# A late pair of loads moved to the weights' queue, and three short matmuls added in the first two tails

## The chip, the cores and the metric

The kernel runs on one core of a Trainium2 chip. Such a core has a matrix engine (TensorE, here PE), a vector engine (VectorE, DVE), a scalar engine (ScalarE, ACT), a general one (GpSimd, POOL) and one that mostly issues transfers (SyncE, SP). Transfers between the chip's large memory and the core run on 16 DMA engines. SP's transfers go through one hardware queue (q1 in the profile), those that POOL issues through a software queue (q0). Matmuls write to a small accumulation memory (PSUM), which ACT and DVE read.

The metric is the time of one execution on the device in microseconds (us), the median of the runs. Lower is better.

## The reference

One layer of a decoder trunk over 512 tokens of width 2048, all in float32. What matters here is its first and its last product:

```python
h = rmsnorm(x, g_mix)
z = einsum('bsd,dc->bsc', h, w_in)          # conv B, C, V | attention Q, K, V | forget logits | two gates
...                                          # gated short convolution and forgetting attention, merged
x = x + einsum('bsd,de->bse', merged, w_mix_out)
h = rmsnorm(x, g_mlp)
u = square(relu(einsum('bsd,df->bsf', h, w_ff1)))     # 2048 -> 8192
x = x + einsum('bsf,fd->bsd', u, w_ff2)               # 8192 -> 2048, "the second MLP matrix"
return rmsnorm(x, g_final)
```

## The kernel before

**Seven products for eight.** Every large product is cut into 2 by 2 blocks and made with seven block products instead of eight (Strassen's scheme in Winograd's form). They are called A11, A12, S1, S2, S3, S4 and A22. Each multiplies a sum of data blocks, which is kept ready in memory, by a sum of weight blocks, which DVE makes when the weights have come.

**Three passes.** Float32 accuracy is had from a shorter format by splitting each operand into a high and a low part. ACT writes the high part (`th`, line 111), DVE the low part (`tl`, line 114), and PE multiplies high by high, high data by low weights or the other way round, and low by high: three matmuls for each pair of blocks. So PE's work on one block product, called a run here, is 48 matmuls of 256 columns, or 24 of 512 columns in the second MLP matrix.

**Two forms.** `mm_cols` (lines 154 to 180) has the weights' parts standing in the array and streams the data through; its three matmuls are lines 171, 175 and 177. `mm_rows` (lines 182 to 201) has the data standing and streams the weights' parts; its matmuls are lines 195, 197 and 199. Both take `extra`. With `extra == "first"` they issue one more matmul of 192 columns ahead of a run's first one, into the same accumulator. It begins the accumulation, and the real first matmul begins it again, so its result is thrown away (line 164 in `mm_cols`, line 193 in `mm_rows`). Some later groups have another kind of short matmul, into a spare bank (line 1058).

**The first stage.** A `Group` is one slab of weight columns with its seven runs: `head` is A11 and A12, `tail2` is S1, S3, S2, S4 and A22 in this order. `heads` is a list of five groups: `gV0`, which makes half of the attention's values and uses `mm_rows`, and four groups for keys and queries, which use `mm_cols` and have `extra={"S3": "first"}`. First all five heads run, then the five tails in the same order. So the first tail is `gV0`'s and the second that of `heads[1]`. Their accumulators are named a, b, c and d: S1 goes to c, S3 to d, S2 to a, S4 to c again, A22 to d again.

**The second MLP matrix.** Its data, the squared activations, are made in the stage before (`ff1`), summed into the seven data blocks and stored to DRAM (`s_d`, lines 1481 and 1482). The last stage reads them back as `us` tiles, at line 1605, in `load_sums`: four tiles for each of eight segments of 1024 rows. For the first segment they take over buffers as the stage before lets go of them: tile 0 (A11, A12) before the last `ff1` group's tail, tile 1 (S2, S3) behind that tail. The last two, tile 2 (S1, A22) and tile 3 (S4), are called the late sums here. They are issued within the first unit, behind its run A12 in the order of the program. Each tile of two blocks is two transfers of 1024 KB, tile 3 two of 512 KB.

A `unit` is one segment by half of the output columns. It loads four weight tiles `y` of 1024 KB on SP (line 1706), in the order (0,0), (1,0), (0,1), (1,1); the fourth is called y11 below. Then it runs A11, A12, S2, S3, S1, A22, S4. Three sums of weights come between: `X[0,1] - X[0,0]`, then `t2 = X[1,1] - ...` for S2, then one for S3.

**Order.** The instructions of each engine run in the order in which a scheduler put them at build time. It follows the program's order as far as it holds a tile's buffers free in time. A transfer is issued by its engine in that order and waits there until its target buffer is free.

Of the kernel before, what the change touches and what calls it, by code (L numbers as in the profile page):

```python
# [8 lines left out]
F32 = mybir.dt.float32  # L9
# [36 lines left out]
def tile_hybrid_block(ctx: ExitStack, tc, x, g_mix, w_in, b_f, b_gate, conv_w, w_conv_out,  # L46
                      w_attn_out, w_mix_out, g_mlp, w_ff1, w_ff2, g_final, out):
    nc = tc.nc
    x, out = x[0], out[0]
# [35 lines left out]
    s_d = [dram.tile([P, 2, 4, 7, HS], F32, name=f"s_d{i}") for i in range(DFF // 1024)]  # L85
# [30 lines left out]
    def split(src, hi, lo):  # L116
        return high_of(src, hi), low_of(src, hi, lo)
# [15 lines left out]
    def parts(shape, at=0):  # L133

        q, w = shape[1:]
        return tuple(main.tile([P, WBUF], F32R, tag=tag, name=tag, bufs=2)[:, at:at + q * w]
                     .rearrange("p (q c) -> p q c", q=q) for tag in ("th", "tl"))
# [44 lines left out]
    def mm_rows(ps, Sx, hi, lo, first, extra=None, blocks=range(2), qs=None):  # L182

        nq, w = hi.shape[1], hi.shape[2]
        for b in blocks:
            o = ps[b][:, :w] if len(ps) == 2 else ps[0][:, b * w:(b + 1) * w]
            begin = first and (b == 0 or len(ps) == 2)
            ts = slice(b * P, (b + 1) * P)
            for part in range(2):
                for q in qs or range(nq):  # L190
                    Sh, Sl = (e[:, ts] for e in Sx(q))
                    if extra == "first" and part == 0 and q == 0 and b == 0:
                        nc.tensor.matmul(o[:, :192], Sh, hi[:, q, :192], start=True, stop=False, skip_group_check=True)
                    if part == 0:
                        tied(nc.tensor.matmul(o, Sh, hi[:, q, :], start=begin and q == 0, stop=False,  # L195
                                              skip_group_check=True))
                        tied(nc.tensor.matmul(o, Sl, hi[:, q, :], start=False, stop=False, skip_group_check=True))  # L197
                    else:
                        tied(nc.tensor.matmul(o, Sh, lo[:, q, :], start=False, stop=q == nq - 1,  # L199
                                              skip_group_check=True))  # L200
# [7 lines left out]
    def moving(t):  # L208

        return lambda q: (t[:, 0, q, :], t[:, 1, q, :])  # L210
# [411 lines left out]
    def store_v(c0, w):  # L622
        def put(i, j, v):
            c = c0 + j * w
            n = min(w, AW - c)
            nc.gpsimd.dma_start(out=v_d[2 * i:2 * i + 2, :, c:c + n].rearrange("t p c -> p t c"), in_=v[:, :, :n])
            if n < w:
                add(fl[:, 2 * i:2 * i + 2, :], v[:, :, n:], bf.unsqueeze(1).to_broadcast([P, 2, NH]))
        return put
# [8 lines left out]
    gV0 = Group(w_in, COL_AV, COL_AV + VW, VW, Q1.moving, mm_rows, ((4,), (3,), (6,), (7,)), store_v(0, VW), shift=3 * SHIFT)  # L638

    def kq(hp, banks):  # L640
        return Group(w_in, COL_K + hp * HS, COL_Q + hp * HS, HS, Q1.moving, mm_cols, banks, store_kq(hp), QSCALE,
                     extra={"S3": "first"})
# [8 lines left out]
    heads = [gV0] + [kq(hp, ((a,), (3,), (6,), (7,))) for hp, a in enumerate((0, 1, 2, 5))]  # L651
# [163 lines left out]

    gV0.after["S2"] = fourth
    gV0.paced = True
    for g in heads:
        g.tail2()
        if g is gV0:  # L820
            ph.close()
# [774 lines left out]

    US = ((4, ("A11", "A12")), (3, ("S2", "S3")), (1, ("S1", "A22")), (2, ("S4",)))

    def load_sums(seg, ks, ST):

        for k in ks:
            place, names = US[k]
            t = main.tile([P, 2, 4, len(names), HS], F32R, tag=f"t{place}", name="us")
            for e in range(2):
                nc.gpsimd.dma_start(out=t[:, e].bitcast(F32), in_=s_d[seg][:, e, :, 2 * k:2 * k + len(names)])
            for e, n in enumerate(names):
                ST[n] = moving(t[:, :, :, e])

    for g in range(1, DFF // S):
        group = ff1(g, ((2 + 2 * (g % 2),), (3,), (1 if g < DFF // S - 1 else 2,), (7,)))  # L1610
        group.head(True, order=((0, 0), (0, 1), (1, 0)))
        if g == DFF // S - 1:
            us0 = {}
# [74 lines left out]
    def banks2(i, name):  # L1688
        return tuple(pairs.tile([P, S], F32, tag=f"q{i}{e}", name=name) for e in range(2))

    def unit(seg, cg, ST):

        a, d = banks2(cg, "a"), banks2(1 - cg, "d")
        if seg == 0:
            kept[cg] = banks2(2 + cg, "b")
        b = kept[cg]
        X, at = {}, {}
        end = seg == NSEG - 1 and cg == 1  # L1700
        for i, j in ((0, 1), (1, 1), (0, 0), (1, 0)) if end else ((0, 0), (1, 0), (0, 1), (1, 1)):
            at[i, j] = free.pop(0)
            t = main.tile([P, 4, S], F32, tag=f"x{at[i, j]}", name=f"y{i}{j}")
            c = NW * cg + S * j
            src = w_ff2[seg * 1024:(seg + 1) * 1024, c:c + S].rearrange("(q two p) c -> two p q c", two=2, p=P)
            nc.sync.dma_start(out=t, in_=src[i])
            X[i, j] = t

        def run(ps, n, src, first):
            hi, lo = parts([P, 4, S])  # L1710
            split(src, hi, lo)
            mm_rows(ps, ST[n], hi, lo, first)

        last = seg == NSEG - 1
        begun = set()

        def into(i, j, ps, end=False):
            for e in range(2):
                xs = place(i, j, cg, e)[2]
                if last and end:  # L1720
                    finish(i, j, cg, ps, e)
                elif seg == 0 and (i, j) not in begun:
                    nc.scalar.activation(out=xs, in_=ps[e], func=AF.Copy)
                elif (i, j, cg) in in_rows:
                    onto_rows(i, j, cg, ps, e)
                else:
                    add(xs, ps[e], xs)
            begun.add((i, j))

        t2 = main.tile([P, 4, S], F32, tag="t0", name="t2")  # L1730
        if end:


            one = const.tile([P, 1], F32, name="one")
            nc.vector.tensor_copy(one, turned[:, 0:1])
            sub(t2, X[1, 1], X[0, 1])
            run(a, "A11", X[0, 0], True)
            onto_rows(0, 0, cg, a, 1)
            onto_rows(0, 0, cg, a, 0, one)
            nc.vector.memset(one, 1.0)  # L1740
            run(d, "S3", t2, True)
            sub(X[0, 0], X[0, 1], X[0, 0])
            sub(X[0, 1], X[1, 1], X[0, 0])
            into(1, 1, d)
            run(a, "S2", X[0, 1], False)
            sub(X[0, 1], X[1, 0], X[0, 1])
            into(1, 0, a)
            for t in (2, 3):
                gain(t, one)
            run(d, "A22", X[0, 1], False)  # L1750
            into(1, 0, d, True)
            run(a, "S1", X[0, 0], False)
            into(1, 1, a, True)
            p4 = (main.tile([P, 4, S], F32R, tag="t0", name="th4"),
                  main.tile([P, 4, S], F32R, tag=f"x{at[0, 1]}", name="tl4"))
            split(X[1, 1], *p4)
            for t in (2, 3):
                Final(t).all()
            p2 = parts([P, 4, S])
            split(X[1, 0], *p2)  # L1760
            for t in (0, 1):
                gain(t, one)
            for e in range(2):
                mm_rows(b, ST["A12"], *p2, False, blocks=(e,))
                finish(0, 0, cg, b, e)
                mm_rows(a, ST["S4"], *p4, False, blocks=(e,))
                finish(0, 1, cg, a, e)
                Final(e).all()
            return
        run(a, "A11", X[0, 0], True)  # L1770
        sub(X[0, 0], X[0, 1], X[0, 0])
        into(0, 0, a)
        run(b, "A12", X[1, 0], seg == 0)
        if seg == 0 and cg == 0:
            load_sums(0, (2, 3), us0)
        if last:
            into(0, 0, b, True)
        sub(t2, X[1, 1], X[0, 0])
        run(a, "S2", t2, False)
        sub(X[0, 1], X[1, 1], X[0, 1])  # L1780
        sub(t2, X[1, 0], t2)
        free.append(at[1, 0])
        into(1, 0, a)
        run(d, "S3", X[0, 1], True)
        free.append(at[0, 1])
        into(1, 1, d)
        run(a, "S1", X[0, 0], False)
        free.append(at[0, 0])
        into(1, 1, a, True)
        run(d, "A22", t2, False)  # L1790
        into(1, 0, d, True)
        run(a, "S4", X[1, 1], False)
        free.append(at[1, 1])
        into(0, 1, a, True)
        if 3 <= seg < 7:
            residual(*((0, 0), (1, 0), (1, 1), (0, 1))[seg - 3], cg)

    kept = {}
    for seg in range(NSEG):
        ST = us0  # L1800
        if seg > 0:
            ST = {}
# [36 lines left out]
```

## Time and profile before

| what | us |
|---|---|
| median of 3 runs (2416.66 to 2418.52) | 2417.17 |
| the profiled execution | 2418.55 |
| its span, first to last instruction | 2416.7 |
| PE busy | 2396.0 (99%) |
| DVE busy | 2029.8 (84%) |
| ACT busy | 1205.1 (50%) |
| mean granted clock of PE | 0.998 |

Rows of a stage table read: stretch, its length, then for PE, PEld (PE's weight loads, which run beside its matmuls), DVE, ACT and POOL the busy time and in brackets the number of instructions, then PE's granted clock, the DMA engines' share and GB/s. Rows of a timeline read: start, duration, engine, line, operation, output and inputs, shapes, count, and in square brackets the idle time before it with what ended it. Rows of the chain read: start, length, what. Groups read: line, engine, operation, output and inputs, shapes, count, busy us, mean ns of one, idle us before them. Ends of matmuls are modelled and overlap with the next start; their starts are measured. Data blocks of the first stage show as A and S, those of w_mix_out as M.

### The profile page before, as it was taken

Reading aid. Unit: us, or ns where it says so; the run is one execution under the profiler, and the core shown is the slowest. Engines: PE = TensorE matmul, PEld = TensorE weight load, DVE = VectorE, ACT = ScalarE, POOL = GpSimd, SP = SyncE. Lnnn points to the kernel's source line nnn. Section 1 sums busy time; section 2 is a strip of 40 time slices with the busy share of each in tenths; the row PEclk is TensorE's granted clock in tenths of the full one; section 3 lists DMA queues with packets and bytes.
Section 4 is the critical chain, followed back from the end, with each engine's and each line's share of the span. In section 5 each row is a group of like instructions: output and inputs, shape, how many; then the busy total and the mean of one; then the engine's idle time right before and its main releaser. Section 6 shows DMA issues by size and latency. Waiting matters only on the chain.

```text
span 2416.7 us, 41351 instructions
## 1 busy us (share of the span) xinstructions
PE 2396.0 (99%) x17775; PEld 2259.7 (94%) x17775; DVE 2029.8 (84%) x1683; ACT 1205.1 (50%) x1238; POOL 300.0 (12%) x480
## 2 busy tenths in 40 slices
PE   9999999999999999999999999999999999999998
PEld 9999999999999999899999999999998888888886
DVE  7987677789888768888988889888887888889898
ACT  7444444445545534446665666666664333333334
POOL 1100111121111112023300000000011001100000
PEclk9999999999999999999999999999999999999999
DMA  8664444464565755566956564655678467665662
GB/s 276 187 189 153 150 154 153 153 205 152 178 201 181 259 176 202 179 193 224 324 184 225 199 231 170 224 206 198 233 288 292 168 210 252 218 212 183 232 231 100
DMA packets 279847, 491.98 MB, mean 204 GB/s; under 512 B 11820, under 2 KB 191112, under 8 KB 279280
## 3 DMA queue, kind: packets, MB, share of 16 engines
q1 hardware_dynamic: 226384, 272.71, 35.6%
q0 software_dynamic: 52672, 215.57, 24.4%
q8 instruction: 139, 2.28, 0.4%
q10 hardware_dynamic: 608, 1.06, 0.1%
q14 instruction: 44, 0.36, 0.0%
HBM read 379.70 MB, written 109.07 MB: 202 GB/s over the span
## 4 chain that ended last, share of the span: by engine, by line
PE 90%; DVE 3%; issue 2%; DMA 2%; ACT 1%; POOL 1%; SPq 0%; POOLq 0%; DVEq 0%; ACTq 0%
PE a L171 6%; PE a L175 6%; PE a L177 6%; PE d L171 5%; PE d L175 5%; PE d L177 5%; PE a L197 5%; PE a L195 5%; PE a L199 5%; PE c L177 4%; PE c L171 4%; PE c L175 4%; PE d L199 3%; PE d L195 3%; PE d L197 3%; PE b L171 3%
## 5 line engine op out<-in xcount | busy, mean ns | idle before, releaser
L111 ACT ACTIVATE th<-x 128x2048 fp32r<-128x2048 f32 (+1 forms) x280 | 537.0, 1918 | 486.6 <-DVE x L128 175.5
L114 DVE TENSOR_TENSOR tl<-x,th 128x2048 fp32r<-128x2048 f32 (+2 forms) x282 | 639.5, 2274 | 152.8 <-ACT th L111 149.1
L128 DVE TENSOR_TENSOR x<-x,x 128x2048 f32<-128x2048 f32 (+1 forms) x160 | 366.1, 2288 | 23.0 <-DMA x<-in_w_in_dram 17.6
L111 ACT ACTIVATE th<-y 128x2048 fp32r<-128x2048 f32 (+1 forms) x109 | 185.3, 1701 | 274.2 <-PE a L197 138.8
L114 DVE TENSOR_TENSOR tl<-y,th 128x2048 fp32r<-128x2048 f32 (+1 forms) x109 | 219.0, 2013 | 28.5 <-ACT th L111 28.1
L195 PE MATMUL a<-th,us 128*128 128x512 f32 x512 | 199.3, 389 | 0.4 <-ACT th L111 0.4
L197 PE MATMUL a<-th,us 128*128 128x512 f32 x512 | 199.2, 389 | 0.0
L171 PE MATMUL c<-S,th 128*128 128x256 f32 x848 | 195.9, 277 | 0.0
L175 PE MATMUL c<-S,th 128*128 128x256 f32 x848 | 195.7, 277 | 0.0
L171 PE MATMUL a<-S,th 128*128 128x256 f32 x784 | 182.3, 278 | 0.0
L175 PE MATMUL a<-S,th 128*128 128x256 f32 x784 | 180.7, 276 | 0.0
L171 PEld LDWEIGHTS c<-S,th 128*128 128x128 f32 x848 | 159.3, 188 | 0.0
L175 PEld LDWEIGHTS c<-S,th 128*128 128x128 f32 x848 | 159.3, 188 | 0.0
L171 PEld LDWEIGHTS a<-S,th 128*128 128x128 f32 x784 | 147.2, 188 | 0.6 <-issue 0.5
L175 PEld LDWEIGHTS a<-S,th 128*128 128x128 f32 x784 | 147.3, 188 | 0.5 <-issue 0.5
L199 PE MATMUL a<-tl,us 128*128 128x512 f32 x512 | 136.9, 389 | 0.6 <-DVE tl L114 0.6
L171 PE MATMUL b<-A,th 128*128 128x256 f32 x544 | 126.0, 277 | 1.4 <-ACT th L111 1.4
L171 PE MATMUL a<-A,th 128*128 128x256 f32 x544 | 126.5, 278 | 0.0
L171 PE MATMUL d<-S,th 128*128 128x256 f32 x544 | 126.4, 278 | 0.0
L175 PE MATMUL d<-S,th 128*128 128x256 f32 x544 | 125.7, 277 | 0.0
L171 PE MATMUL d<-A,th 128*128 128x256 f32 x544 | 125.7, 277 | 0.0
L175 PE MATMUL b<-A,th 128*128 128x256 f32 x544 | 125.5, 277 | 0.0
(401 smaller groups left out, 6030.7 us busy)
## 6 DMA issues: line engine op xcount, KB each, us to landing
x<-in_w_in_dram SPq DMA_DIRECT2D x86, 1024.0 KB, 5.9
y<-in_w_ff_dram SPq DMA_DIRECT2D x64, 1024.0 KB, 7.5
x<-in_w_ff_dram SPq DMA_DIRECT2D x60, 1024.0 KB, 8.2
us<-s_d POOLq DMA_DIRECT2D x48, 1024.0 KB, 9.2
s_d<-rh POOLq DMA_DIRECT2D x32, 896.0 KB, 5.4
s_d<-r POOLq DMA_DIRECT2D x32, 896.0 KB, 5.9
x<-in_w_mix_out_dram SPq DMA_DIRECT2D x17, 1024.0 KB, 6.9
g_d<-o POOLq DMA_DIRECT2D x32, 256.0 KB, 2.9
```

The source lines that it names most:

```text
L111: return tied(nc.scalar.activation(out=hi, in_=src, func=AF.Copy))
L114: return tied(nc.vector.tensor_tensor(out=lo, in0=src, in1=hi.bitcast(F32), op=ALU.subtract))
L128: return nc.vector.tensor_tensor(out=out, in0=a, in1=b, op=ALU.subtract)
L171: i = nc.tensor.matmul(o, hi[:, q, js], Sh, start=first and q == 0 and j == 0, stop=False, skip_group_check=True)
L175: nc.tensor.matmul(o, hi[:, q, js], Sl, start=False, stop=False, skip_group_check=True)
L177: i = nc.tensor.matmul(o, lo[:, q, js], Sh, start=False, stop=q == nq - 1, skip_group_check=True)
L195: tied(nc.tensor.matmul(o, Sh, hi[:, q, :], start=begin and q == 0, stop=False, skip_group_check=True))
L197: tied(nc.tensor.matmul(o, Sl, hi[:, q, :], start=False, stop=False, skip_group_check=True))
L199: tied(nc.tensor.matmul(o, Sh, lo[:, q, :], start=False, stop=q == nq - 1, skip_group_check=True))
```

## The change

Two edits. The first adds `extra` to the first two tails: to `gV0` for S1 and S3, and to `heads[1]` for S1 (it has S3 already). That is three more matmuls of 192 columns, the first two of them in `mm_rows`. The second passes a queue to `load_sums` and uses SP for the late sums of the first segment, four transfers; all other `us` loads stay on POOL.

```diff
     gV0.after["S2"] = fourth
     gV0.paced = True
+    gV0.extra = {"S1": "first", "S3": "first"}
+    heads[1].extra = {"S1": "first", "S3": "first"}
     for g in heads:
         g.tail2()
...
-    def load_sums(seg, ks, ST):
+    def load_sums(seg, ks, ST, queue=nc.gpsimd):
 
         for k in ks:
             place, names = US[k]
             t = main.tile([P, 2, 4, len(names), HS], F32R, tag=f"t{place}", name="us")
             for e in range(2):
-                nc.gpsimd.dma_start(out=t[:, e].bitcast(F32), in_=s_d[seg][:, e, :, 2 * k:2 * k + len(names)])
+                queue.dma_start(out=t[:, e].bitcast(F32), in_=s_d[seg][:, e, :, 2 * k:2 * k + len(names)])
...
         run(b, "A12", X[1, 0], seg == 0)
         if seg == 0 and cg == 0:
-            load_sums(0, (2, 3), us0)
+            load_sums(0, (2, 3), us0, nc.sync)
```

## The prediction

> **What bounds the kernel now.** I read the page first: engine shares, then the chain that ended last.
>
> ```profile
> span 2416.7 us, 41351 instructions
> PE 2396.0 (99%) x17775; PEld 2259.7 (94%) x17775; DVE 2029.8 (84%) x1683; ACT 1205.1 (50%) x1238; POOL 300.0 (12%) x480
> PE 90%; DVE 3%; issue 2%; DMA 2%; ACT 1%; POOL 1%; SPq 0%; POOLq 0%; DVEq 0%; ACTq 0%
> ```
>
> TensorE (PE) is the chain for 90% of the span. So the time can fall in two ways only: matmuls follow each other faster, or PE waits less. The change touches one place of each kind. Both are small, and I look at each with the views of its own stretch.
>
> The first place is the pace. The stage table (length, then PE's busy time with its count) holds stretches that are each one run of 48 matmuls of 256 columns; each begins and ends where the timeline starts a new output. The last four rows come from a second and a third table.
>
> ```profile
> 70.85:76.29 5.44, 5.44 (x50) 5.44 (x49) 5.44 (x3) 0.84 (x2) 0.00 (x0) 1.00 0.67 198
> 76.29:81.95 5.66, 5.66 (x51) 5.66 (x49) 4.16 (x4) 1.92 (x1) 0.71 (x1) 1.00 0.13 46
> 110.31:115.98 5.67, 5.67 (x50) 5.67 (x49) 4.62 (x3) 3.56 (x2) 0.00 (x0) 1.00 0.69 217
> 132.94:138.59 5.65, 5.65 (x50) 5.65 (x49) 5.38 (x4) 0.40 (x2) 1.27 (x2) 1.00 0.39 118
> 138.68:144.17 5.49, 5.49 (x51) 5.49 (x50) 4.21 (x2) 3.28 (x2) 0.57 (x1) 1.00 0.81 242
> 144.17:149.61 5.44, 5.44 (x51) 5.44 (x50) 2.89 (x2) 2.45 (x3) 0.00 (x0) 1.00 0.88 256
> 477.75:483.19 5.44, 5.44 (x51) 5.44 (x50) 5.44 (x5) 3.49 (x2) 0.00 (x0) 1.00 0.66 190
> 483.19:488.74 5.55, 5.55 (x52) 5.55 (x50) 5.19 (x6) 1.50 (x4) 0.00 (x0) 1.00 0.79 217
> 76.29:138.59 62.30, 62.30 (x531) 62.30 (x530) 54.04 (x32) 25.94 (x19) 9.17 (x11) 1.00 0.57 174
> 1800.16:1819.00 18.84, 17.20 (x73) 13.28 (x72) 17.49 (x14) 10.94 (x11) 1.11 (x2) 1.00 0.86 296
> ```
>
> The same work takes 5.44 us in one stretch and 5.65 in another, at the full clock (1.00) and with PE never idle: 113.3 or 117.8 ns a matmul. The slow pace begins at 76.29, where the first tail begins, and lasts over both first tails and one run more, 11 runs, to 138.59. Just there stands a short matmul (192 columns) that the kernel already has:
>
> ```profile
> 110.22 0.25 PE L164 MATMUL d<-S,th 128*128 128x192 f32 x1
> 138.59 0.25 PE L164 MATMUL d<-S,th 128*128 128x192 f32 x1
> ```
>
> The one at 110.22 left the pace slow (5.67 behind it), the one at 138.59 ended it (5.49, then 5.44). The groups of 461 to 843 us hold twelve more (ten L1058, two L164), and there nothing is slow: modelled matmuls of 276 ns, against 281 in the two first tails.
>
> ```profile
> L175 PE MATMUL c<-S,th 128*128 128x256 f32 x320 | 73.5, 276 | 0.0
> L1058 PE MATMUL spare<-S,th 128*128 128x192 f32 x10 | 2.5, 248 | 0.0
> L175 PE MATMUL c<-S,th 128*128 128x256 f32 x48 | 11.4, 281 | 0.0
> ```
>
> The second place is a real wait. In the first unit of the second MLP matrix three runs take 18.84 us (last row of the table) where three at 5.44 are 16.32: 2.52 us lost. The chain says to what:
>
> ```profile
> 1784.15 2.30 DVE tl L114
> 1786.47 15.33 DMA y<-in_w_ff_dram
> 1801.82 0.04 DVE t L128
> ...
> 1812.91 2.29 DVE tl L114
> 1815.25 1.20 PE d L199 x4
> ```
>
> The unit's fourth weight tile y11 is 15.33 us on its way, VectorE (DVE) starts S2's sum when it lands, and from there DVE is back to back until PE has what it waited for.
>
> **The change part by part: the three short matmuls.** Price of one: 483.19 to 488.74 is 48 matmuls with a short one ahead, 5.55 against 5.44, so 0.11 us on PE's path; three cost 0.33. Nothing hides it. The weight loads they bring run beside (PEld), and no wait is added: each needs only what the next matmul needs.
>
> Gain, if the pace becomes fast at the first of them: 62.30 less the 0.11 of the short one it holds, less 11 x 5.44, is 2.35 us. Net -2.02. If only the second (first tail, S3) does it, 0.21 less. If only the third or the old one at 110.22 does it, 6 or 5 runs of 0.21 remain: -0.93 or -0.72 net. If none, +0.33. No row shows a short matmul in the row form (gV0's, data as moving operand) nor one where the form changes, so its result is bounded by these: from -2.02 to +0.33, and further up if the later rescue is lost (below). I take -2.02. Twelve short matmuls met a fast pace and left it fast; the first new one stands right behind a fast run (70.85 row). Row-form matmuls can run fast, as those of w_mix_out do (mean 276, in 1065 to 1076 us):
>
> ```profile
> L195 PE MATMUL d<-th,M 128*128 128x256 f32 x16 | 3.7, 276 | 0.0
> ```
>
> Cover when PE gets faster: DVE is the next engine, 54.04 of 62.30 us. At 11 x 5.44 plus four short ones PE needs 60.3, so DVE still fits, and the tails behind 138.59 run at the fast pace with the same DVE work and no wait.
>
> [...]
>
> **The late sums.** POOL (GpSimd) issues them now, and SP (the weights' queue) after the change. Four issues leave POOL, four come onto SP. The listing of POOL, then DVE around the wait, then the issue views of y11, of the early pair and of the S1/A22 pair:
>
> ```profile
> 1784.27 1.52 POOL L1605 DMA_DIRECT2D us<-s_d  x2 [0.48 <-PE d L177]
> 1789.71 1.50 POOL L1605 DMA_DIRECT2D us<-s_d  x2 [3.92 <-PE a L177]
> 1795.15 1.49 POOL L1605 DMA_DIRECT2D us<-s_d  x2 [3.94 <-PE d L177]
> 1808.01 0.56 POOL L1481 DMA_DIRECT2D s_d<-rh  x1 [11.37 <-ACT rh L1478]
> 1801.82 2.29 DVE L128 TENSOR_TENSOR t<-y,y 128x2048 f32<-128x2048 f32 x1 [1.17 <-DMA y<-in_w_ff_dram]
> DMA to landing us min/median/max: 15.3/15.3/15.3
> L1605 POOL DMA_DIRECT2D us<-s_d x2: 766/766/766, 1784.3 to 1785.0; - x2
> DMA to landing us min/median/max: 12.3/14.1/15.8
> DMA to landing us min/median/max: 13.7/14.7/15.7
> ```
>
> SP: y11 is issued at 1786.47; the new loads wait for PE at 1789.71 and 1795.15. Behind them SP has the next unit's weights, which wait for a free buffer until 1813.06:
>
> ```profile
> L1706 SPq DMA_DIRECT2D y<-in_w_ff_dram x1: 368/368/368, 1813.1 to 1813.1; - x1
> ```
>
> 18 us lie between, so the added waits hold up nobody. On POOL the next work waits for ScalarE (ACT) at 1808: nothing is won there.
>
> What y11 wins: in 1790 to 1798 the software queue q0 moved twice what q1 (weights) did, and in 1798 to 1802 q1 finished y11 beside it.
>
> ```profile
> q0 software_dynamic: 539, 2.12, 68.1%
> q1 hardware_dynamic: 493, 0.99, 33.8%
> ...
> q0 software_dynamic: 357, 1.36, 89.8%
> q1 hardware_dynamic: 105, 0.18, 12.9%
> ```
>
> But until about 1800.8 (second early load, issued at 1785.0, 15.8 us on its way) q0 still carries the early pair, which stays on POOL. Only the last 1.0 us of y11 (1800.8 to 1801.8) competes with the late sums alone, at a third of the rate; alone it takes a third, 0.33. Gain 0.67. Upper bound: DVE was idle 1.17 us before that sum and not longer. Lower: 0. I take 0.65, the slowest engine's view, since a landing counts only when all are done. DVE's chain passes it on: S2's th, its tl and S3's tl (1815.2) all come 0.65 earlier, and PE's last wait there (1815.25) is set by that tl. The remaining 1.9 us of waiting stay. The S1/A22 pair lands by 1806.2 now (second issue 1790.5, 15.7 us); S1 starts at 1819, so it has 13 us to spare on either queue.
>
> [...]
>
> Sum: -2.02 - 0.65 = -2.67. The profiled execution took 2418.55 us (span 2416.7 and 1.85 around it), 1.38 above the median 2417.17. It becomes 2415.9, the median 2414.5.
>
> **The rivals.** (a) The pace is mended only from the second tail on: -0.93 or -0.72, with the loads -1.4 to -1.6, 2415.7. For it: the first tail is where it broke (76.29), at the change of form, so the same break may follow the short matmul; the one at 110.22 failed. (b) No new short matmul mends it: +0.33 - 0.65, 2416.9. For it: one of two failed in a slow stretch. Against: four tries instead of one ahead of 138.59. (c) Slower: the short matmuls shift the pattern, the pace stays slow, and the one at 138.59 now fails as that at 110.22 did. Then 14 more runs to the end of the heads lose 0.21 each: +2.98 + 0.33 - 0.65, 2419.8. It is slower as soon as two more runs are lost. Against it: four chances to fail in a row, and the later heads have two more short ones. (d) The scheduler puts the first late pair ahead of y11 on SP: y11 is issued after 1789.7 and has the pair's 2.1 MB ahead of it; at most 1.36 MB of them passed beside it till now, so 0.74 MB come on top, 1.9 us at the 389 GB/s of both queues, and PE waits so much longer: with the pace mended -0.1, 2417.1. Against: y11's buffer is free 3.2 us before theirs.
>
> **How the numbers follow.** Forecast 0.50, (a) 0.20, (b) 0.18, (c) 0.06, (d) 0.06. Time 2414.5. Low end: the whole of 2.02 and nearly the whole wait of 2.52 gone, 2412.6, less a little for the median, 2412.4. High end: no pace mended and nothing won by the loads, 2417.5, and 0.7 for the spread of the three runs, 2418.2; beyond it lies (c). The forecast's own range is 2413.4 (DVE's 1.17) to 2415.2. A change under 0.2% (4.8 us) cannot be told from none here; the two places hold 2.02 + 2.52 = 4.54 together, so faster by more is 0.08, slower by more 0.04.
>
> **What would show it.** Right: runs of 5.44 from the first tail on, 138.59 reached some 2 us earlier; y11 on its way about 14.7 us; the waits of PE in the first unit near 1.9 us. Wrong: 5.65 in the first tails; a late sum ahead of y11; DVE in another order, which the changed issue times could bring anywhere.

## The result and the profile after

| | before | after |
|---|---|---|
| median (runs side by side, 22 of each), us | 2418.98 (2414.80 to 2423.50) | 2414.41 (2411.24 to 2416.70) |
| the profiled execution, us | 2418.55 | 2415.49 |
| its span, us | 2416.7 | 2413.4 |

The ratio of the times is 0.998, with a 95% interval of 0.9974 to 0.9986: 3.4 to 6.3 us faster. The forecast was 2414.5. But the 22 runs of the kernel before lie 1.8 us above the median of three that the forecast started from, so the change won more (4.57 between the medians) than the 2.67 that it was given: that the forecast is met to 0.1 us is luck, two misses of 1.8 and 1.9 that cancel. Where did the gain come from? Stretch by stretch of the two profiled executions:

| stretch, by PE's starts | before | after | difference |
|---|---|---|---|
| start to the heads' first run | 32.79 | 32.81 | +0.02 |
| four heads and two tails, to heads[2]'s S3 | 105.80 | 104.06 | -1.74 |
| from there to the first unit | 1656.10 | 1655.41 | -0.69 |
| first unit, to its S1 | 24.31 | 23.74 | -0.57 |
| from there to the span's end | 597.72 | 597.41 | -0.31 |

**The pace.** The stage table of the kernel after, each row but the last three one run of 48 matmuls (the second and third with the short one ahead of it):

```profile
70.88:76.32 5.44, 5.44 (x51) 5.44 (x49) 5.44 (x3) 0.84 (x2) 0.00 (x0) 1.00 0.67 198
76.32:81.88 5.56, 5.56 (x51) 5.56 (x50) 4.06 (x4) 1.92 (x1) 0.71 (x1) 1.00 0.14 48
81.88:87.44 5.56, 5.56 (x52) 5.56 (x50) 5.53 (x3) 3.22 (x2) 0.00 (x0) 1.00 0.38 97
103.85:109.53 5.68, 5.68 (x51) 5.68 (x50) 5.47 (x4) 1.17 (x1) 2.22 (x3) 1.00 0.36 134
109.61:115.11 5.50, 5.50 (x51) 5.50 (x50) 4.56 (x3) 3.50 (x2) 0.00 (x0) 1.00 0.77 237
32.81:136.87 104.06, 104.06 (x919) 104.06 (x918) 97.21 (x54) 51.31 (x37) 12.09 (x15) 1.00 0.63 194
1792.28:1816.02 23.74, 22.55 (x99) 17.79 (x97) 23.53 (x19) 14.83 (x17) 1.11 (x2) 1.00 0.94 327
1797.75:1816.02 18.27, 17.08 (x74) 13.28 (x72) 18.06 (x15) 11.30 (x12) 1.11 (x2) 1.00 0.91 309
```

The first short matmul makes the first tail fast: 5.56 with it, where 5.66 stood without. At 103.85 the form changes back from rows to columns, and there the run is slow (5.68) though the third new short matmul stands right ahead of it. The old one behind that run mends it (5.50, then 5.44). The same two stretches before:

```profile
32.79:138.59 105.80, 105.80 (x915) 105.80 (x914) 97.49 (x55) 51.52 (x38) 12.06 (x15) 1.00 0.62 192
1794.69:1819.00 24.31, 22.67 (x98) 17.79 (x97) 22.96 (x19) 14.83 (x17) 2.60 (x4) 1.00 0.90 317
```

**The first unit.** The three runs behind A11, which are A12, S2 and S3 (last row of the first table), take 18.27 us instead of 18.84: PE loses 1.95 instead of 2.52. PE's waits in the unit, before and then after (engine, line, what it waited for, us, times, longest):

```profile
PE a L199 <- DVE tl L114: 0.6, 1, 0.6
PE d L199 <- DVE tl L114: 0.6, 1, 0.6
PE a L195 <- ACT th L111: 0.4, 1, 0.4
```

```profile
PE a L199 <- DVE tl L114: 0.6, 1, 0.6
PE d L199 <- DVE tl L114: 0.6, 1, 0.6
```

The wait for S2's `th` at the end of A12 is gone. The issue view of y11 and DVE's timeline after:

```profile
L1708 SPq DMA_DIRECT2D y<-in_w_ff_dram x1: 367/367/367, 1784.1 to 1784.1; - x1
...
DMA to landing us min/median/max: 14.3/14.3/14.3
```

```profile
1792.20 2.29 DVE L128 TENSOR_TENSOR y<-y,y 128x2048 f32<-128x2048 f32 x1 [2.13 <-DMA y<-in_w_ff_dram]
...
1798.48 0.42 DVE L128 TENSOR_TENSOR r<-r 128x256 f32<-128x256 f32 x1
1798.81 2.29 DVE L128 TENSOR_TENSOR t<-y,y 128x2048 f32<-128x2048 f32 x1
```

S2's sum (1798.81) has no idle time before it any more; y11 is 14.3 us on its way, 1.0 less. What is late now is the tile ahead of it, the third one (y01): DVE waits 2.13 us for it, where it waited 1.46 before:

```profile
1793.95 2.29 DVE L128 TENSOR_TENSOR y<-y,y 128x2048 f32<-128x2048 f32 x1 [1.46 <-DMA y<-in_w_ff_dram]
```

The chain says the same. It now begins with the issue of y01 (1778.62), not of y11:

```profile
1778.62 13.49 DMA y<-in_w_ff_dram
...
1792.20 0.10 DVE y L128
...
1809.98 2.21 DVE tl L114
...
1812.23 1.20 PE d L199 x4
```

**The middle**, which the change doesn't touch, differs by 0.69. There the execution before has one place of its own, in w_mix_out, where PE waited for a transfer (the waits of 1080 to 1100 us, then the stage table):

```profile
PE d L195 <- ACT th L111: 2.6, 1, 2.6
```

```profile
1088.00:1090.00 2.00, 0.31 (x3) 0.11 (x1) 0.69 (x1) 1.53 (x2) 0.69 (x2) 1.00 1.07 406
1090.00:1092.00 2.00, 1.04 (x9) 1.05 (x10) 1.07 (x1) 2.00 (x5) 0.54 (x1) 1.00 0.84 329
1092.00:1094.00 2.00, 2.00 (x13) 2.00 (x12) 1.97 (x3) 2.00 (x3) 0.00 (x0) 0.58 0.17 66
1094.00:1096.00 2.00, 2.00 (x12) 2.00 (x11) 2.00 (x2) 1.43 (x5) 0.71 (x1) 0.56 0.69 161
```

Behind the wait the granted clock is 0.58 and 0.56 over some 4 us, which costs 1.7 more. In the profile after, the same wait is 1.1 us and the clock stays full there. The edits did not bring it: of the eight profiles of the two unchanged programs it came in one of each. The execution after gave most of that back by the pace: its twelve runs from 1244 to 1313 were slow, and the same twelve were fast in the execution before. One of them, before and then after:

```profile
1281.86:1287.30 5.44, 5.44 (x51) 5.44 (x49) 4.38 (x3) 4.04 (x4) 1.06 (x2) 1.00 1.06 363
1278.14:1283.80 5.66, 5.66 (x51) 5.66 (x49) 4.23 (x2) 3.99 (x4) 1.07 (x2) 1.00 1.02 326
```

Counted by the starts of the matmuls, the middle holds 28.5 runs' worth of slow matmuls before and 43.9 after, 6.1 and 9.3 us. No edit touches them.

### The profile page after: what moved, and what is told of

The parts are those of the page before. It is cut to its first block, busy times and chain, and to the rows that moved or that the text cites. A ratio compares the mean times of both kernels' runs of the same rounds, so it can differ in the third digit from the quotient of the medians.

```text
span 2413.4 us, 41364 instructions
## 1 busy us (share of the span) xinstructions
PE 2396.1 (99%) x17778; PEld 2259.7 (94%) x17778; DVE 2029.7 (84%) x1683; ACT 1205.2 (50%) x1238; POOL 297.8 (12%) x476
## 5 line engine op out<-in xcount | busy, mean ns | idle before, releaser
L171 PE MATMUL a<-A,th 128*128 128x256 f32 x544 | 126.8, 279 | 0.0
L171 PE MATMUL d<-S,th 128*128 128x256 f32 x544 | 126.3, 278 | 0.0
L175 PE MATMUL a<-A,th 128*128 128x256 f32 x544 | 125.7, 277 | 0.0
```

Source lines behind the costliest of these rows:

```text
L171: i = nc.tensor.matmul(o, hi[:, q, js], Sh, start=first and q == 0 and j == 0, stop=False, skip_group_check=True)
L175: nc.tensor.matmul(o, hi[:, q, js], Sl, start=False, stop=False, skip_group_check=True)
```

## The experiments

The theory: the first short matmul ends the slow pace at the change of form, and in the first unit y11 comes earlier once the late sums no longer compete with it. The rival for the unit: what PE wins earlier is lost again there, since the tiles come no earlier. Each part alone was run first.

**E1, only the short matmuls.** Against the kernel after:

```diff
-            load_sums(0, (2, 3), us0, nc.sync)
+            load_sums(0, (2, 3), us0)
```

> The three short matmuls alone, the late sums stay on POOL. Theory (the pace): the first tail starts its runs at 5.44-5.47 us, one run of the second tail stays at 5.65, the short matmul of heads[2] starts 1.7 us earlier than before (138.59), and the three runs in the first unit of the second MLP matrix take the same 18.8 us as before; alone this is worth -1.7 us. Rival 1 (the tails got faster for another reason, for instance the changed issue order): 62.3 us in the tails again. Rival 2 (the short matmuls also bring the gain that the profiles show between 840 and 1800 us): the median is 3 us or more below the kernel before.

2417.27 (11 runs), ratio 0.9991 (0.9982 to 1.0). Heads and tails take 104.05, as in the kernel after. But the first unit takes 26.81, 2.5 more than before:

```profile
33.51:137.56 104.05, 104.05 (x919) 104.05 (x917) 97.27 (x54) 51.28 (x37) 12.07 (x15) 1.00 0.63 192
1792.66:1819.47 26.81, 23.03 (x98) 17.72 (x97) 23.70 (x19) 14.82 (x17) 2.60 (x4) 1.00 0.80 288
```

That speaks for the rival, and E6 and E9 to E12 ask whether it belongs to the kernel.

**E2, only the loads.** Against the kernel after:

```diff
-    gV0.extra = {"S1": "first", "S3": "first"}
-    heads[1].extra = {"S1": "first", "S3": "first"}
```

> The late sums on SP alone, no new short matmuls. Theory: the tails take 62.3 us as before, the three runs in the first unit 18.2 to 18.3 us (0.6 less), y11 is 14.7 us on its way; alone this is worth -0.6 us. Rival (the changed issue order alone moves the stages between 840 and 1800 us): more than 2 us between this kernel and the one before, with both places as the theory has them.

2417.76 (11 runs), ratio 0.9994 (0.9985 to 1.0003). The tails are slow as before, the unit is 0.89 shorter. By its time alone neither part is clear of no change; each shows in its own stretch:

```profile
32.82:138.62 105.80, 105.80 (x915) 105.80 (x914) 97.48 (x55) 51.49 (x38) 12.07 (x15) 1.00 0.62 192
1794.87:1818.29 23.42, 22.38 (x98) 17.88 (x97) 23.24 (x19) 14.82 (x17) 1.11 (x2) 1.00 0.93 330
```

**E3, the kernel before again**, unchanged.

> The kernel before once more, for what two executions of one kernel differ by. If the stages between 840 and 1800 us wander by themselves, their starts differ from the first profile's by 1 us or more, while 76 to 138 us and the first unit of the second MLP matrix repeat to 0.1 us. If they repeat to 0.3 us, the 0.7 us that the changed kernel gained there belongs to the change. Time: no difference.

2418.18 (10 runs), ratio 0.9999 (0.999 to 1.0008). Its profile shows a picture that nobody had expected:

```profile
72.81:78.47 5.66, 5.66 (x51) 5.66 (x50) 5.06 (x3) 1.28 (x3) 0.00 (x0) 1.00 0.59 175
78.47:83.93 5.46, 5.46 (x51) 5.46 (x50) 4.65 (x3) 1.44 (x1) 0.71 (x1) 1.00 0.14 48
100.24:105.69 5.45, 5.45 (x51) 5.45 (x50) 4.49 (x3) 2.41 (x3) 1.08 (x2) 1.00 0.82 241
105.69:111.34 5.65, 5.65 (x51) 5.65 (x50) 5.03 (x3) 1.25 (x1) 1.56 (x3) 1.00 0.31 102
33.27:138.68 105.41, 105.41 (x916) 105.41 (x914) 97.47 (x54) 51.19 (x37) 12.06 (x15) 1.00 0.62 189
```

Here the eight runs of the heads go at the slow pace, 5.65 us each, and the change of form at 78.47 makes the pace fast. So at the change of form the runs went from 5.44 to 5.66 us in the profile before (76.29) and from 5.66 to 5.46 here, and the sum is nearly the same (105.41 against 105.80). The pace need not flip there: where the rows were slow, the columns behind them stayed slow (5.66 from 104.56 in the profile before).

**E4, the early pair on SP as well** (kernel after, and tile 1 moved too).

```diff
-    load_sums(0, (1,), us0)
...
-            load_sums(0, (2, 3), us0, nc.sync)
+            load_sums(0, (1, 2, 3), us0, nc.sync)
```

> The changed kernel with the early pair (S2, S3) on SP behind the fourth weight tile too. Theory (what is left of y11's delay is the early pair on the software queue): y11 is 9 to 11 us on its way, the fourth sum no longer waits, PE's waits in the first unit fall from 1.9 to under 0.5 us, and the kernel gains 1 to 1.5 us on the changed one; the early pair lands about 1.5 us before S2 needs it. Rival 1 (the rest of the wait is DVE's own chain): y11 earlier, the waits as they are, no gain. Rival 2 (the early pair lands too late): S2 waits for it, some us slower.

2411.60 (7 runs, 2411.08 to 2413.03), ratio 0.9969 (0.9959 to 0.998). The unit and all of PE's waits in it:

```profile
1790.26:1812.81 22.55, 22.10 (x99) 17.95 (x98) 22.35 (x19) 14.84 (x17) 1.06 (x2) 1.00 0.97 340
```

```profile
PE d L199 <- DVE tl L114: 0.4, 1, 0.4
```

y01 is 12.3 us on its way and y11 12.2 (9 to 11 had been expected), though the scheduler put the early pair's first transfer ahead of y11 in the queue. That order was rival (d) for the late sums, where 1.9 us of loss were estimated; here it brought none, which speaks for the software queue beside SP's as what counts. This version beats the kernel before clearly. Its median is also 2.8 us below that of the kernel after, but the two were not run side by side, and their ratios to the kernel before have overlapping intervals.

**E5, one short matmul instead of three** (loads as after).

```diff
-    gV0.extra = {"S1": "first", "S3": "first"}
-    heads[1].extra = {"S1": "first", "S3": "first"}
+    gV0.extra = {"S1": "first"}
```

> Loads as in the changed kernel; of the three short matmuls only the first (gV0, S1, where the row form begins) is kept. If one short matmul at the change of form is enough, the runs of both first tails up to heads[1]'s S1 take 5.44 to 5.47 us, as in the changed kernel, heads[1]'s S1 (first run in column form again) is slow at 5.65 to 5.68, the old short matmul in S3 mends it, and heads[2]'s S3 begins 1.75 + 0.2 = 1.95 us ahead of the kernel before. If the second is needed to hold the pace, the second run or one after it goes back to 5.65, and 0.2 us are lost for each such run up to the next short matmul. If the eight runs of the heads ahead of it are slow themselves (as in the second run of the kernel before, 5.65 from 33 to 78 us), the start counts from there. Time about 2414.5.

```profile
76.45:82.02 5.57, 5.57 (x52) 5.57 (x50) 4.07 (x4) 1.92 (x1) 0.71 (x1) 1.00 0.14 48
82.02:87.46 5.44, 5.44 (x51) 5.44 (x49) 5.41 (x3) 3.10 (x2) 0.00 (x0) 1.00 0.35 89
103.78:109.43 5.65, 5.65 (x50) 5.65 (x49) 5.62 (x5) 1.26 (x1) 2.22 (x3) 1.00 0.44 163
32.95:136.77 103.82, 103.82 (x916) 103.82 (x915) 97.09 (x54) 51.32 (x37) 12.08 (x15) 1.00 0.63 192
```

One is enough, in this one profile. The other two cost 0.12 each and win nothing: 103.82 against 104.05. The time (2420.07, one run) is high by things elsewhere: its unit took 25.53, and its middle 1658.36, with the low clock in w_mix_out and the slow pace from 1247 to 1315.

**E6, the short matmuls alone, again.**

> Again the three short matmuls without the moved loads, for the first unit of the second MLP matrix. If the 5.0 us that PE waited there in the first such run belong to the kernel (PE comes about 2 us earlier, the tiles do not), PE again waits 4 to 5.5 us in the three runs, and the time is near 2417. If one late DMA engine was the chance of that run, the wait is back near 2.5 us and the time 2 us lower, near 2415. The tails as in the changed kernel: 5.44 to 5.47 but for one run.

104.05 in heads and tails, 27.23 in the unit; 2416.55 in its one run.

**E7, the kernel after again.**

> The changed kernel itself once more. If its first profile shows what the change does, the eight runs of the heads and the first tails are at 5.44 again, heads[2]'s S3 begins about 136.9 us, y11 is 14 to 15 us on its way, and PE waits 1.9 us or less in the first unit; time 2412 to 2416. If the pace of the heads is chance (slow in the second run of the kernel before), they may take 5.65 each, the tails 5.44 behind them, and heads[2]'s S3 begins 1.7 us later, near 138.6: then the short matmuls gain nothing in such a run.

104.05 and 25.30; 2417.76, one run. PE's wait in the three runs was 3.5 us, not the 1.9 that was hoped for. The tails repeat exactly, the unit doesn't.

**E8, short matmuls where they might serve**, on top of E4.

```diff
+    keys.extra = {"A11": "first", "S3": "first"}
...
-    heads[1].extra = {"S1": "first", "S3": "first"}
+    gV1.extra = {"A11": "first"}
```

> The version with the early pair of sums in the weights' queue too, and the short matmuls where the runs showed a use: gV0's S1 and S3 as in the changed kernel, none in heads[1]'s S1 (which stayed slow with it: 0.11 us back), one at the head of heads[1]'s A11 (the first of the heads' eight runs, so that they can't start slow) and one at the head of gV1's A11 (seven runs of 48 x 260 columns at 5.77 us, 120.2 ns, where 260/256 of 113.3 would be 115.1). If the 120.2 is the slow pace, those seven runs fall to 5.52, 1.7 us less; if it is simply the price of 260 columns, they stay at 5.77 and 0.11 us are lost. PE's wait in the first unit about 0.8 us. Time 2411.6 if 260 columns cost what they cost, 2410 if not; ratio 0.9969 or 0.9962 to the kernel before.

2412.87 (7 runs), ratio 0.997 (0.9959 to 0.9981), not to be told from E4. The runs of 260 columns (the first with the short one) stay at 5.77:

```profile
214.09:219.90 5.81, 5.81 (x51) 5.81 (x50) 5.16 (x3) 1.36 (x3) 0.73 (x1) 1.00 0.14 52
219.90:225.67 5.77, 5.77 (x51) 5.77 (x49) 2.66 (x2) 2.26 (x3) 0.00 (x0) 1.00 0.00 0
```

So the 120.2 ns there are no slow pace that this short matmul ended. The unit takes 22.38, as in E4.

**E9 to E12, the kernels before and after, twice more each**, unchanged.

> The kernel before once more, for two questions. (1) The pace: the heads' eight runs (33 to 76 us) were fast in seven of the eight profiles of kernels without a short matmul at their head, and slow (5.65 each) in one of the kernel before; where they were slow, the first tail came out fast, and the sum to heads[2]'s S3 was the same (138.6 to 138.7). Expected: either picture, with 138.6 in both. (2) The first unit: in the three profiles with the old matmuls y10 was 8.0 to 8.8 us on its way and PE waited 1.4 to 2.2 us; in four of five with new short matmuls, the early pair on POOL, y10 took 11.0 us. If the short matmuls bring that, y10 takes 8 to 9 us here; if it is chance, 11.0 comes up here too, with a wait of 4 to 5 us and a time near 2421.

> The changed kernel a third time. Tails as before in it (5.44 to 5.47, one run of 5.68). y10: if the short matmuls bring the late DMA engine, 11.0 us in most such profiles and PE's wait in the first unit about 3 us, time near 2416; if chance, as often 8 to 9 us, wait 1.5 us, time near 2414.

> The kernel before a fourth time, same two questions: the pace of the heads either way with heads[2]'s S3 at 138.6; y10 at 8 to 9 us if the late engine comes with the short matmuls, at 11.0 in about half if it is chance.

> The changed kernel a fourth time: tails at 5.44 to 5.47 but one; y10 at 11.0 us if the late engine comes with the short matmuls, else as often at 8 to 9.

One run each: 2422.43 and 2418.78 before, 2417.29 and 2415.33 after. y10 took 11.2 and 11.1 us in the two of before, 11.7 and 11.0 in the two of after. E9, the kernel before, the issue view of y10, PE's waits in the first unit, and the unit:

```profile
L1706 SPq DMA_DIRECT2D y<-in_w_ff_dram x1: 367/367/367, 1778.1 to 1778.1; - x1
...
DMA to landing us min/median/max: 11.2/11.2/11.2
```

```profile
PE a L195 <- ACT th L111: 2.2, 1, 2.2
PE b L199 <- DVE tl L114: 0.7, 1, 0.7
...
```

```profile
1795.77:1822.89 27.12, 22.97 (x99) 17.72 (x98) 23.70 (x19) 14.84 (x17) 2.61 (x4) 1.00 0.78 284
```

So the long unit comes in the kernel before too: the rival falls, and E1's long unit was no price of the short matmuls. Sorted by y10's flight, the unit takes:

| y10 on its way | late sums on POOL | late sums on SP |
|---|---|---|
| 8.0 to 8.8 us | 24.31, 24.39 (before, E3) | 23.74, 23.42 (after, E2) |
| 11.0 to 11.7 us | 26.81, 27.23, 27.12, 26.54 (E1, E6, E9, E11) | 25.53, 25.30, 26.44, 25.26 (E5, E7, E10, E12) |

The moved loads win 0.6 to 1.0 us in the first row and about 1.3 in the second (means 26.9 and 25.6), from two and four profiles a side; E10's 26.44 and E11's 26.54 all but meet. E11's is no pure case: its PE waited 2.2 us once, as in E1 and E9, but then had the low clock (0.94 over the unit, where those two had 1.00). Plainer is y11's own flight: 15.3 to 18.2 us in the six profiles with the late sums on POOL, 14.3 to 15.0 in these six with them on SP.

## Why the prediction was right

**The short matmuls: right in mechanism, 0.27 too much.** Predicted -2.02. In the two unchanged programs heads and tails together took 105.80, 105.41, 105.81 and 105.80 before, and 104.06, 104.05, 104.05 and 104.06 after: -1.75 where the heads are fast, -1.35 against E3. The step that was mis-sized is "11 x 5.44": ten runs became fast. The eleventh, heads[1]'s S1 at the change from rows to columns, stays slow (0.21, and 0.03 behind its short one). I had named this for the first tail, in rival (a), and not for the second change of form. The other 0.03 is the price: 0.12 each. That the pace would be fast from the first tail on held, in all nine profiles with a short matmul there. Whether those tails would have been slow without it depends on the heads: in one of five profiles without it they were not, and no profile of the changed kernel shows what it does behind slow heads.

**The loads: the size right by luck, the step not.** Predicted -0.65 and a remaining wait of 1.9; measured -0.57 and 1.95. But the working had y11 land 0.67 earlier and PE keep all of it. Relative to the unit's start y11 landed 1.0 earlier and DVE's whole 1.17 of idle time went: "competes with the late sums alone" for the last 1.0 us was priced too low. (That a landing counts only when all are done the profile before bears out: 102 of q1's packets end from 1798 to 1800.8, three more by 1801.4, none from there on, and y11 lands at 1801.80.) That the late sums take nothing from y11 once they stand behind it on SP was my estimate, and no run shows it: from 1792.0 to 1798.4 in the profile after, when y11 lands, q1 moved 1.41 MB, of which y11 is 1.05 at most. The unit kept only half, because y01 landed 0.7 later against the same start (0.8 ahead of it before, 0.2 after), and from y01 on DVE is back to back. So the upper bound for y11 was reached, and "the remaining 1.9 us stay" hides that the cause had moved one tile ahead. The two errors cancel. Why y01 came later than before is not shown: y10, ahead of it in the queue, took 0.7 longer too (8.7 against 8.0), so it may be the variation of these flights and not the change. That the early pair on the software queue has a part in it E4 shows: with the pair on SP y01's wait falls to 0.94 and the unit to 22.55.

```profile
1789.00 2.29 DVE L128 TENSOR_TENSOR y<-y,y 128x2048 f32<-128x2048 f32 x1 [0.94 <-DMA y<-in_w_ff_dram]
```

**Where the rest of the medians' 4.6 comes from.** Tails 1.35 to 1.75, unit 0.6 to 1.3 and 0.3 at the end make 2.2 to 3.4; the larger sum all but reaches the near end of the measured 3.4 to 6.3. The mean spans of four profiles of each kernel differ by 3.3 (2417.7 and 2414.4). The untouched middle varies by itself, 1654.1 to 1656.3 before and 1653.0 to 1655.9 after, which is more than what is left; its means differ by 0.9.

What varies there can be read from the starts of the matmuls. Over all fourteen profiles the middle takes 1652.7 to 1658.4. In it the slow pace costs 5.6 to 9.3 us (26 to 44 runs' worth), PE's idle time 4.6 to 8.2, and the low clock 1.7 in three profiles (before, E5, E7). With these three taken off, 1640.2 to 1642.0 remain. Some slow stretches stand in every profile (near 1010 to 1055, eight runs); others come and go in one kernel, as the twelve runs near 1244 to 1313: slow in the profile after, in E3 and in E5, fast in the other eleven. What decides that is open.

The 0.3 at the end lies behind the last issue (4.74 us to the span's end before, 4.43 after) and came in every profile with the late sums on SP: 597.3 to 597.4 from S1 on, against 597.7 to 597.8. Most of it (0.24) stands behind the last landing, where SP goes through the program's closing waits one by one, 0.06 us each: seven of them are left there before (2415.47 to 2415.86), three after (2412.41 to 2412.56). The prediction had nothing for it.

**What did not happen.** Rival (b) is out by the tails, (c) by the run behind 136.87 (5.47), and (d) by the order: the late sums stand behind y11 on SP and land behind it (1801.22 the first, y11 1798.34). SP's new waits delayed nothing that PE needed, as priced: from S1 on the kernel takes 597.41 us, before 597.72.

## What to carry to other kernels

Cost a stall by the tile ahead of it too: here y11 landed 1.0 us earlier and the unit kept 0.57, because y01, one tile ahead in the same chain, came 0.7 later. Where equal runs go at two paces (here 5.44 and 5.65 us), count the matmuls of each pace over the whole kernel, look for the places where the kind of operand changes, and try one cheap disturbance there before three (here 103.82 us with one short matmul, 104.05 with three). Before an effect of 2 us in one profile is given to an edit, take the unchanged kernel's profile a few times: here the unit of the kernel before took 24.3 and 27.1 us with nothing changed, and the untouched middle moved by 2.

## What was not expected of the hardware

- The pace of equal matmuls, 113.3 or 117.8 ns, held over many runs: eight in the heads, eleven in the first tails before, twelve from 1244 to 1313 after. The change from rows to columns made a fast pace slow in all ten profiles where it met one (5.68 us a run in the profile after, 5.65 in E3 and E5), and left a slow one slow in the other four (5.66 in the profile before); the change from columns to rows made a fast one slow (5.66, the profile before) and, in E3, a slow one fast (5.46). A short matmul at the first change of form kept or made the pace fast in nine profiles (heads and tails 103.82 to 104.06 in all nine); at the second it did not. Inside one form it ended a slow pace at 138.59 before and at 109.53 after, and left it slow at 110.22 before, in all four profiles with slow rows. In the middle's stretch of twelve at the slow pace it was the same in all three profiles: the first short matmul in it (1272.38 in the profile after) left the pace slow, the second (1312.07) ended it. So one short matmul is no sure cure. What sets the pace was not found, and whether an extra matmul of another length would do the same was not tried.
- One transfer of 1 MB in the same place takes 8.0 to 8.8 us or 11.0 to 11.7, within one kernel: 8.0, 8.3, 11.2 and 11.1 in the four profiles of the kernel before. In the 0.8 us that begin 5.1 us behind the issue of the unit's first weights, three packets of the software queue still ended in E9 and one in E11, both late, and none in the profiles before and after. I read that as a small part of the DMA engines beginning late; no run shows it, for no view here names an engine, and what delays the transfer was not found. E9 to E12 all came out late (11.0 to 11.7), so it may not fall anew at each execution.
- After one idle time of PE the granted clock fell to about a half for 3.4 us (0.50 from 1092.5 to 1095.5 in the profile before, 0.83 and 0.76 in the half microsecond ahead of it and behind it): behind 2.6 us of idleness in the profile before, 2.0 in E5, 2.2 in E11 and 1.8 in E7, but not behind 2.2 in E1 and E9, nor in E6 (1.00 over the unit in all three). Why equal idle times differ in what follows, no run here shows. The rows of E11:

```profile
1804.00:1806.00 2.00, 0.11 (x1) 0.00 (x0) 2.00 (x3) 1.60 (x1) 0.00 (x0) 1.00 0.62 217
...
1808.00:1810.00 2.00, 2.00 (x5) 1.23 (x5) 2.00 (x2) 2.00 (x2) 0.56 (x1) 0.50 0.40 168
1810.00:1812.00 2.00, 2.00 (x8) 1.58 (x8) 2.00 (x2) 0.78 (x2) 0.56 (x1) 0.78 0.73 290
```
